# Two token mixers: softmax scaling on ScalarE, softmax steps by column, and the S5 states' products in another place and order

## The chip, the cores and the metric

The kernel runs on one core of a Trainium2 chip, as one program with one launch. The metric is the device time of one execution in microseconds. The profile records one execution on the chip: what each engine ran, when, and what it waited for. The engines are TensorE (PE in the profile, its weight loads PEld), VectorE (DVE), ScalarE (ACT), GpSimd (POOL) and SyncE (SP), which here only issues transfers.

## The reference

A trunk of two layers works on 256 latent tokens and 256 context tokens of 1024 features. Each layer is a SwiGLU half-step, a token mixer, and another SwiGLU half-step, each between two RMS norms with a shift, a scale and a gate from a conditioning vector. Only the latent tokens are returned, so the second layer computes less for the context. The mixer is what the change touches:

```
q, k, v, u, gb, gc, z = split(h @ w_in)
# attention: 8 heads in 2 groups, window of 128 and all context, a sink per head
p = softmax(concat([s_loc, s_ctx, sink])); out = p[..., :-1] @ v
# S5: 16 groups of 64 complex states, both directions
s[t] = a * s[t-1] + B u[t];  y = Re(C s) + d * u
g = gelu(y);  ssm = g * sigmoid(g @ w_glu + b_glu)
# short convolution: gb * conv3(gc * z)
y = concat([attn, ssm, conv]) @ w_out
```

## The kernel before

Features lie on the 128 partitions, tokens along the free axis: columns 0 to 255 are context, 256 to 511 latent. Large products are made from fp32 values split into a high and a low part (`wsplit` for weights, `split` for activations): ACT casts the high part, DVE or POOL subtracts for the low part (L134, L143), and PE runs three matmuls per tile (L156).

A mixer is a list of small steps, `PROG[l]`, run in the order written by hand. PE executes in exactly that order. The other engines' instructions are ordered by a scheduler when the program is built, from its own estimate of times and from their order in the program. The steps that matter here: `t` input projection tiles, `s0`/`s1` the S5 states of group half 0 and 1 (`ssm_states`), `o` their output (`ssm_out`), `b` the way back to features with GELU (`ssm_back`), `g` the gate (`ssm_glu`), `S` scores and softmax of an attention unit (`attn_s`), `T` its transposes, which wait for the scaled probabilities, `V` the product with the values, and `e` pieces of the output projection. A unit is a pair of heads with one tile of 128 latent queries (n = 1, two columns of row statistics) or the whole context (n = 2, four columns). The first mixer has 12 units, 4 of them with four columns; the second has 8 with two.

An attention unit runs on DVE: two maxima (L1166), m, nm and es (L1170 to L1174); on ACT: an exponential for es and one for each part with its sum (L1175, L1182); then on DVE again sm, its reciprocal, and the scaling of P (L1185 to L1192). An S5 state runs: PE makes two products in PSUM (pe), ACT copies them to SBUF (tx, L1047), DVE and POOL rotate them with tables co and si (L1058 to L1060, POOL into one tile tz), DVE scans (L1063), and DVE and POOL rotate back (L1068 to L1075). POOL can't read PSUM. POOL also subtracts the low parts of the output projection's weights (L134) and runs parts of the convolution (L1265 to L1273).

PSUM tiles of 128x512 come from two pools, `mm` with six banks (scores S, pe, projections, gate) and `ms` with two. The tables co, si and rho of each state (tiles tvv and tt) are loaded by SP's queue, which also carries all weights, in order.

Of the kernel before, what the change touches and what calls it, by code (L numbers as in the profile page):

```python
# [12 lines left out]
AF = mybir.ActivationFunctionType  # L13
OP = mybir.AluOpType
# [14 lines left out]
SCALE = 64 ** -0.5  # L29
# [49 lines left out]
class Trunk:  # L79
# [140 lines left out]
    def setup2(self):  # L220

        nc, a = self.nc, self.a
        self.ropec = self.cst("ropec", [128, 2, 256])
        nc.sync.dma_start(self.ropec, a["k_rope"])
        tri = self.slot("tri")[:, :256].rearrange("p (i c) -> p i c", i=2)
        nc.sync.dma_start(tri, a["k_tri"])
        self.misc = self.cst("misc", [128, NL, 24])
        nc.sync.dma_start(self.misc, a["misc"])
        self.par = self.cst("par", [128, 3, NL * 16])
        nc.sync.dma_start(self.par, a["ssm_par"])  # L230
        self.ssmd = self.cst("ssmd", [128, NL, 4])
        nc.sync.dma_start(self.ssmd, a["ssm_d"])
        self.mask16 = self.cst("mask16", [128, 16])
        nc.sync.dma_start(self.mask16, a["k_mask16"])
        self.ij = self.cst("ij", [64, 128])
        nc.sync.dma_start(self.ij, a["k_ij"])
        self.trib = self.cst("trib", [128, 2, 128], BF16)
        nc.vector.tensor_copy(self.trib, tri)
        bg = self.misc[:, :, 16:18]
        nc.vector.tensor_scalar(bg, bg, 0.5, None, op0=OP.mult)  # L240


    def conditioning(self):
# [603 lines left out]
    def ssm_tables(self, l):  # L847
# [6 lines left out]
        for gh in range(2):  # L854
# [3 lines left out]
            for i in range(3):  # L858
                self.R[l, gh, i] = dr("R", 512)

# [171 lines left out]
    def ssm_states(self, l, gh, U):  # L1032

        nc = self.nc
        v = nc.vector
        E = []
        for ri in range(2):
            w = self.wraw(self.W[l, gh, ri])
            p = self.ps("pe")
            for i in range(8):  # L1040
                for d in range(2):
                    hf = slice(64 * d, 64 * d + 64)
                    nc.tensor.matmul(p[hf, i * 64:(i + 1) * 64], w[:, i * 128 + 64 * d:i * 128 + 64 * d + 64],
                                     U[8 * gh + i][:, 64 * d:64 * d + 64], start=True, stop=True,
                                     skip_group_check=True, tile_position=(0, 64 * d))
            e = self.own("tx", 2)
            nc.scalar.activation(e, p, AF.Copy)  # L1047
            E.append(e)
        R = []
        for i in range(3):  # L1050
            r = self.own("tvv", 2) if i < 2 else self.own("tt")
            nc.sync.dma_start(r, self.R[l, gh, i])
            R.append(r)
        co, si, rho = R
        tt = [self.own("tw"), self.own("tz")]
        X = [self.own("tc"), self.own("tpw")]
        for i, (s0, s1, o) in enumerate(((0, 1, OP.add), (1, 0, OP.subtract))):
            v.tensor_tensor(tt[0], E[s0], co, op=OP.mult)  # L1058
            nc.gpsimd.tensor_tensor(tt[1], E[s1], si, op=OP.mult)
            v.tensor_tensor(X[i], tt[0], tt[1], op=o)  # L1060
        Y = [self.own(f"tbb{i}") for i in range(2)]
        for i in range(2):
            v.tensor_tensor_scan(Y[i], rho, X[i], 0.0, op0=OP.mult, op1=OP.add)  # L1063
        S = [self.slot("S") for _ in range(2)]
        z = lambda x: x.rearrange("p (g c) -> p g c", c=64)
        f, r = slice(0, 64), slice(64, 128)
        for i, (s0, s1, o) in enumerate(((0, 1, OP.subtract), (1, 0, OP.add))):
            v.tensor_tensor(tt[0], Y[s0], co, op=OP.mult)  # L1068
            nc.gpsimd.tensor_tensor(tt[1], Y[s1], si, op=OP.mult)
            s, t0, t1 = z(S[i]), z(tt[0]), z(tt[1])  # L1070
            v.memset(s[f, :, 0:1], 0.0)
            v.memset(s[r, :, 31:32], 0.0)
            v.tensor_tensor(s[f, :, 1:64], t0[f, :, 0:63], t1[f, :, 0:63], op=o)
            v.tensor_tensor(s[r, :, 30::-1], t0[r, :, 0:31], t1[r, :, 0:31], op=o)
            v.tensor_tensor(s[r, :, 63:31:-1], t0[r, :, 31:63], t1[r, :, 31:63], op=o)  # L1075
        return S
# [26 lines left out]
    def ssm_back(self, yt, lo):  # L1103

        nc = self.nc
        cl = lo // CH
        n = 64 - cl
        p = self.ps("pyt")
        pv = p.rearrange("p (c j) -> p c j", j=CH)
        for j in range(CH):  # L1110
            for q in range(128 // n):
                c = slice(n * q, n * q + n)
                nc.tensor.matmul(pv[c, cl:, j], yt[c, j * n:j * n + n], self.ident[c, c], start=True, stop=True,
                                 skip_group_check=True, tile_position=(n * q, n * q))
        g = self.slot("gelu")[:, lo:]
        x = p[:, lo:]
        nc.scalar.activation(g, x, AF.Square)
        nc.vector.tensor_scalar(g, g, 0.044715, 1.0, op0=OP.mult, op1=OP.add)
        nc.vector.tensor_tensor(g, g, x, op=OP.mult)
        nc.scalar.activation(g, g, AF.Tanh, scale=math.sqrt(2.0 / math.pi))  # L1120
        nc.vector.scalar_tensor_tensor(g, g, 1.0, x, op0=OP.add, op1=OP.mult)
        return g

    def ssm_glu(self, l, G, cat, lo):

        nc = self.nc
        wg = self.slot("wglu")
        nc.sync.dma_start(wg, self.a["w_glu"][l])
        for half in range(2):
            p = self.ps("pglu")  # L1130
            for k in range(2):
                nc.tensor.matmul(p[:, lo:], wg[:, k * 256 + half * 128:k * 256 + half * 128 + 128], G[k],
                                 start=k == 0, stop=k == 1)
            o = self.slot("sg")[:, lo:]
            nc.scalar.activation(o, p[:, lo:], AF.Tanh, bias=self.misc[:, l, 16 + half:17 + half], scale=0.25)
            nc.vector.scalar_tensor_tensor(o, o, 1.0, G[half], op0=OP.add, op1=OP.mult)
            ch, cl = self.slot("xh", F32R), self.slot("xl", F32R)
            nc.scalar.activation(ch[:, lo:], o, AF.Copy, scale=0.25)
            nc.vector.scalar_tensor_tensor(cl[:, lo:], o, 0.25, ch.bitcast(F32)[:, lo:], op0=OP.mult, op1=OP.subtract)
            cat[6 + half] = ch, cl  # L1140


    def attn_s(self, l, i, q, k, qt):
        nc = self.nc
        S = [self.ps("S") for _ in range(2)]
        for part in ((qt,) if qt is not None else (0, 1)):
            for ab in range(2):
                pr = slice(64 * ab, 64 * ab + 64)
                if qt is not None:
                    o, qo = S[ab], CTX + qt * 128  # L1150
                else:
                    o, qo = S[ab][:, part * 256:part * 256 + 256], part * 128
# [4 lines left out]
        if qt is not None:  # L1157
            c = 384 if qt == 0 else 256
# [3 lines left out]
        n = 1 if qt is not None else 2  # L1162
        w = 512 // n
        mx = self.tiny("mx", 4)
        for ab in range(2):
            nc.vector.tensor_reduce(mx[:, n * ab:n * ab + n], S[ab].rearrange("p (n k) -> p n k", n=n), axis=AX.X,  # L1166
                                    op=OP.max)
        sink = self.misc[:, l, 4 * i:4 * i + 2 * n] if n == 2 else self.misc[:, l, 4 * i:4 + 4 * i:2]
        m = self.tiny("m", 4)[:, :2 * n]
        nc.vector.scalar_tensor_tensor(m, mx[:, :2 * n], SCALE, sink, op0=OP.mult, op1=OP.max)  # L1170
        nm = self.tiny("nm", 4)[:, :2 * n]
        nc.vector.tensor_scalar(nm, m, -1.0, None, op0=OP.mult)
        es = self.tiny("es", 4)[:, :2 * n]
        nc.vector.tensor_tensor(es, sink, m, op=OP.subtract)  # L1174
        nc.scalar.activation(es, es, AF.Exp)  # L1175
        sm = self.tiny("sm", 4)[:, :2 * n]
        Pm = []
        for ab in range(2):
            P = self.slot("P")
            for z in range(n):  # L1180
                j = ab * n + z
                nc.scalar.activation(P[:, z * w:(z + 1) * w], S[ab][:, z * w:(z + 1) * w], AF.Exp, bias=nm[:, j:j + 1],  # L1182
                                     scale=SCALE, accum_out=sm[:, j:j + 1])
            Pm.append(P)
        nc.vector.tensor_tensor(sm, sm, es, op=OP.add)  # L1185
        rd = self.tiny("rd", 4)[:, :2 * n]
        nc.vector.reciprocal(rd, sm)
        for ab in range(2):
            for z in range(n):
                j = ab * n + z  # L1190
                o = Pm[ab][:, z * w:(z + 1) * w]
                nc.vector.tensor_scalar(o, o, rd[:, j:j + 1], None, op0=OP.mult)  # L1192
        return Pm

    def attn_t(self, Pm, qt):
# [436 lines left out]
```

## Time and profile before

| | us |
|---|---|
| median of 3 runs | 1827.9 (1822.71 to 1828.61) |
| the profiled execution | 1825.46 |
| its span, first to last instruction | 1823.6 |
| TensorE busy in it | 1718.3 |
| VectorE busy in it | 1140.4 |

The first mixer lies at about 480 to 680 us of the span, the second at about 1480 to 1625. Busy time of an engine includes the time in which an instruction that has begun is held up by another engine. A row of a timeline gives the start in us, the duration in us, the engine, the line of the kernel, the operation, the tile written and the tiles read, and in brackets the idle time of the engine before it and what ended it. A row of waits says which instruction waited for which, how long in total, how often and the longest. A row of windows gives the stretch and its length, then the busy us (and instructions) of PE, PEld, DVE, ACT and POOL, the granted clock of TensorE as a share of full speed, the share of DMA in use and GB/s.

### The profile page before, as it was taken

The numbers are of one execution on the slowest core, as the hardware profiler recorded it, in microseconds if no ns is written. First come the engines' busy times: TensorE is split into PE (matmuls) and PEld (weight loads), VectorE is DVE, ScalarE is ACT, GpSimd is POOL, SyncE is SP. The second block draws the span as 40 slices with busy tenths as digits, with TensorE's granted clock in tenths as the row PEclk, the third lists the DMA queues.
The fourth block names the chain that finished last, engine by engine and source line by source line (L and its number), as shares of the span: only waits on it lengthen the run. The fifth ranks groups of instructions, "written<-read, shape, count | busy, mean of one in ns | idle before, by whom it ended". The sixth has DMA issues, their size and how long they took to land.

```text
span 1823.6 us, 28595 instructions
## 1 busy us (share of the span) xinstructions
PE 1718.3 (94%) x11040; PEld 1477.6 (81%) x11040; DVE 1140.4 (63%) x2209; ACT 660.9 (36%) x1173; POOL 712.6 (39%) x623
## 2 busy tenths in 40 slices
PE   7999988999997989999999999999999988889998
PEld 5887776899975889787888999888888977679997
DVE  5798786737489666787774276765365576852223
ACT  4332222234335454323222243422222443545443
POOL 4100886864444143553438343000001562435552
PEclk9999998999998999999999999999999999899999
DMA  7676555644144031656664332646367434445552
GB/s 281 224 226 182 187 176 175 216 146 130 36 145 145 24 93 54 199 181 204 182 193 157 91 116 81 231 139 197 115 209 233 130 104 133 147 138 186 184 186 92
DMA packets 103481, 285.94 MB, mean 157 GB/s; under 512 B 19904, under 2 KB 27152, under 8 KB 103344
## 3 DMA queue, kind: packets, MB, share of 16 engines
q1 hardware_dynamic: 102992, 283.91, 49.4%
q8 instruction: 87, 1.43, 0.3%
q14 instruction: 50, 0.41, 0.1%
q0 software_dynamic: 64, 0.12, 0.0%
q10 hardware_dynamic: 288, 0.07, 0.0%
HBM read 270.45 MB, written 15.70 MB: 157 GB/s over the span
## 4 chain that ended last, share of the span: by engine, by line
PE 70%; DVE 13%; DMA 5%; issue 5%; POOL 4%; ACT 3%; SPq 0%; DVEq 0%; ACTq 0%; POOLq 0%
PE pgu L156 33%; PE pd L156 17%; PE sk L156 7%; PE yr L493 4%; DMA wr<-in_w_ada_dram 4%; PE po L156 2%; DVE junk L249 2%; DVE wl L134 2%; ACT wh L131 1%; PE pgu L544 1%; DMA wr<-in_wgu_dram 1%; PE O L1218 1%; PE ss L341 1%; ACT hh L369 1%; DVE tn L367 1%
## 5 line engine op out<-in xcount | busy, mean ns | idle before, releaser
L134 POOL TENSOR_TENSOR wl<-wr,wh 128x1024 fp32r<-128x1024 f32 (+1 forms) x140 | 326.3, 2347 | 681.7 <-ACT wh L131 299.1
L131 ACT ACTIVATE wh<-wr 128x1024 fp32r<-128x1024 f32 (+2 forms) x350 | 342.2, 983 | 628.6 <-PE pgu L156 167.0
L156 PE MATMUL pgu<-hh,wh 128*128 128x512 f32 (+1 forms) x1296 | 468.7, 362 | 0.0
L156 PE MATMUL pgu<-hl,wh 128*128 128x512 f32 (+1 forms) x1296 | 464.9, 359 | 0.2 <-DVE hl L1473 0.2
L156 PE MATMUL pgu<-hh,wl 128*128 128x512 f32 (+1 forms) x1296 | 464.9, 359 | 0.0
L249 DVE SCALAR_TENSOR_TENSOR junk<-wr,sb 128x1024 bf16<-128x1024 f32 x224 | 312.4, 1395 | 162.3 <-DMA wr<-in_w_ada_dram 160.1
L134 DVE TENSOR_TENSOR wl<-wr,wh 128x1024 fp32r<-128x1024 f32 (+1 forms) x210 | 250.4, 1195 | 70.6 <-ACT wh L131 69.5
L156 PEld LDWEIGHTS pgu<-hh,wh 128*128 128x128 f32 x1296 | 244.6, 189 | 40.4 <-issue 1.7
L156 PEld LDWEIGHTS pgu<-hl,wh 128*128 128x128 f32 x1296 | 244.5, 189 | 39.4 <-DVE hl L1473 0.5
L156 PEld LDWEIGHTS pgu<-hh,wl 128*128 128x128 f32 x1296 | 244.4, 189 | 39.0
L156 PE MATMUL pd<-xh,wh 128*128 128x512 f32 (+1 forms) x696 | 243.5, 350 | 6.9 <-ACT xh L617 6.9
L156 PE MATMUL pd<-xl,wh 128*128 128x512 f32 (+1 forms) x696 | 239.3, 344 | 1.4 <-DVE xl L618 1.4
L156 PE MATMUL pd<-xh,wl 128*128 128x512 f32 (+1 forms) x696 | 239.0, 343 | 0.0
L156 PEld LDWEIGHTS pd<-xh,wh 128*128 128x128 f32 x696 | 132.6, 190 | 25.1 <-ACT xh L617 8.2
L156 PEld LDWEIGHTS pd<-xl,wh 128*128 128x128 f32 x696 | 132.4, 190 | 19.3 <-DVE xl L618 2.7
L156 PE MATMUL sk<-hh,wh 128*128 128x256 f32 x480 | 141.2, 294 | 6.2 <-ACT hh L369 6.2
L156 PE MATMUL sk<-hl,wh 128*128 128x256 f32 x480 | 139.8, 291 | 6.8 <-DVE hl L372 6.8
L156 PEld LDWEIGHTS pd<-xh,wl 128*128 128x128 f32 x696 | 132.4, 190 | 16.1
L156 PE MATMUL sk<-hh,wl 128*128 128x256 f32 x480 | 138.9, 289 | 0.0
L156 PEld LDWEIGHTS sk<-hl,wh 128*128 128x128 f32 x480 | 94.6, 197 | 8.5 <-DVE hl L372 8.3
L156 PEld LDWEIGHTS sk<-hh,wh 128*128 128x128 f32 x480 | 94.6, 197 | 7.9 <-ACT hh L369 7.8
L617 ACT ACTIVATE xh<-pgu 128x512 fp32r<-128x512 f32 (+1 forms) x61 | 35.1, 575 | 169.8 <-DVE pgu L616 169.5
(375 smaller groups left out, 2474.1 us busy)
## 6 DMA issues: line engine op xcount, KB each, us to landing
wr<-in_wgu_dram SPq DMA_DIRECT2D x170, 512.0 KB, 4.2
wr<-in_w_ada_dram SPq DMA_DIRECT2D x144, 512.0 KB, 4.3
wr<-in_wd_dram SPq DMA_DIRECT2D x72, 320.0 KB, 3.2
wr<-in_w_in_dram SPq DMA_DIRECT2D x32, 512.0 KB, 3.9
wr<-in_wd_dram SPq DMA_DIRECT2D x36, 448.0 KB, 3.5
wr<-in_wdr_dram SPq DMA_DIRECT2D x22, 512.0 KB, 3.7
wr<-in_w_out_dram SPq DMA_DIRECT2D x10, 512.0 KB, 4.6
V<-tvv SPq DMA_DIRECT2D x16, 256.0 KB, 2.5
```

Of the source, the lines that this page charges most:

```text
L131: nc.scalar.activation(h[:, :cols], w[:, :cols], AF.Copy)
L134: eng.tensor_tensor(lo[:, :cols], w[:, :cols], h.bitcast(F32)[:, :cols], op=OP.subtract)
L156: mm = lambda a_, x_, st, sp: nc.tensor.matmul(po, a_[:, c], x_[:, lo:hi], start=st, stop=sp, skip_group_check=True)
L249: self.nc.vector.scalar_tensor_tensor(self.junk, w, 1.0, self.sb[:, s], op0=OP.mult, op1=OP.mult, accum_out=self.mod[l][:, m, b, s:s + 1])
L341: self.nc.tensor.matmul(p[:, b:b + 1], t[:, lo + b * 128:lo + (b + 1) * 128], self.rf[:, 0:1], start=first and b == 0, stop=last, skip_gro ...
L367: nc.vector.scalar_tensor_tensor(sc[d % 3], self.x[d][:, lo:hi], self.gs[l][s_][:, d, s:s + 1], rb[:, :hi - lo], op0=OP.mult, op1=OP.mult)
L369: nc.scalar.activation(H[d][0][:, lo:hi], sc[d % 3], AF.Identity, bias=bs[d])
L493: mm = lambda x_, a_, st, sp: self.nc.tensor.matmul(p, x_[:, c], a_[:, o:o + 512], start=st, stop=sp, skip_group_check=True)
L544: nc.tensor.matmul(ps[i // 2][:, o:o + 128], w[:, k * 128:k * 128 + 128], U[k][:, t * 128:t * 128 + 128], start=t + n + i % 2 == 0, stop=n ...
L617: nc.scalar.activation(gh[:, lo:hi], pu, AF.Copy)
L1218: nc.tensor.matmul(O[pr, :w], vt[:, kt * 128 + 64 * ab:kt * 128 + 64 * ab + 64], PT[ab][:, kt * w:(kt + 1) * w], start=kt == 0, stop=kt == ...
```

## The change

In `attn_s` the sinks are negated once at set-up; nm is made directly as the smaller of -SCALE times the maximum and the negated sink, es as nm minus that, and nm, es and sm are made column by column with per-row operands. es is exponentiated after the probabilities, and the probabilities are multiplied by the reciprocal sum on ACT. In `ssm_states` POOL makes both of its first products in two tiles, DVE multiplies co into the products in PSUM and combines there; the rotation back runs for the imaginary part first, with two pairs of tiles, and POOL's product stands first. In `ssm_back` the constant of the GELU is folded into the square, so that one DVE pass less is left, and in `ssm_glu` the gate is worked out in PSUM.

```diff
@@ setup2
         nc.vector.tensor_scalar(bg, bg, 0.5, None, op0=OP.mult)
+        sk = self.misc[:, :, :16]
+        nc.vector.tensor_scalar(sk, sk, -1.0, None, op0=OP.mult)
@@ ssm_states
             nc.scalar.activation(e, p, AF.Copy)
             E.append(e)
+            pe.append(p)
...
         tt = [self.own("tw"), self.own("tz")]
         X = [self.own("tc"), self.own("tpw")]
-        for i, (s0, s1, o) in enumerate(((0, 1, OP.add), (1, 0, OP.subtract))):
-            v.tensor_tensor(tt[0], E[s0], co, op=OP.mult)
-            nc.gpsimd.tensor_tensor(tt[1], E[s1], si, op=OP.mult)
-            v.tensor_tensor(X[i], tt[0], tt[1], op=o)
+        for i in range(2):
+            nc.gpsimd.tensor_tensor(tt[i], E[1 - i], si, op=OP.mult)
+        for i, o in enumerate((OP.add, OP.subtract)):
+            v.tensor_tensor(pe[i], pe[i], co, op=OP.mult)
+            v.tensor_tensor(X[i], pe[i], tt[i], op=o)
...
-        for i, (s0, s1, o) in enumerate(((0, 1, OP.subtract), (1, 0, OP.add))):
-            v.tensor_tensor(tt[0], Y[s0], co, op=OP.mult)
-            nc.gpsimd.tensor_tensor(tt[1], Y[s1], si, op=OP.mult)
+        for i, o, tags in ((1, OP.add, ("tw", "tz")), (0, OP.subtract, ("tc", "tpw"))):
+            tt = [self.own(t) for t in tags]
+            nc.gpsimd.tensor_tensor(tt[1], Y[1 - i], si, op=OP.mult)
+            v.tensor_tensor(tt[0], Y[i], co, op=OP.mult)
@@ ssm_back
-        nc.scalar.activation(g, x, AF.Square)
-        nc.vector.tensor_scalar(g, g, 0.044715, 1.0, op0=OP.mult, op1=OP.add)
-        nc.vector.tensor_tensor(g, g, x, op=OP.mult)
+        nc.scalar.activation(g, x, AF.Square, scale=math.sqrt(0.044715))
+        nc.vector.scalar_tensor_tensor(g, g, 1.0, x, op0=OP.add, op1=OP.mult)
@@ ssm_glu
-            o = self.slot("sg")[:, lo:]
-            nc.scalar.activation(o, p[:, lo:], AF.Tanh, bias=self.misc[:, l, 16 + half:17 + half], scale=0.25)
+            o = p[:, lo:]
+            nc.scalar.activation(o, o, AF.Tanh, bias=self.misc[:, l, 16 + half:17 + half], scale=0.25)
@@ attn_s
-        m = self.tiny("m", 4)[:, :2 * n]
-        nc.vector.scalar_tensor_tensor(m, mx[:, :2 * n], SCALE, sink, op0=OP.mult, op1=OP.max)
-        nm = self.tiny("nm", 4)[:, :2 * n]
-        nc.vector.tensor_scalar(nm, m, -1.0, None, op0=OP.mult)
-        es = self.tiny("es", 4)[:, :2 * n]
-        nc.vector.tensor_tensor(es, sink, m, op=OP.subtract)
-        nc.scalar.activation(es, es, AF.Exp)
...
+        for c in cols:
+            nc.vector.tensor_scalar(nm[:, c], mx[:, c], -SCALE, sink[:, c], op0=OP.mult, op1=OP.min)
+        for c in cols:
+            nc.vector.tensor_scalar(es[:, c], nm[:, c], sink[:, c], None, op0=OP.subtract)
+        Pm = [self.slot("P") for _ in range(2)]
+        part = lambda j: Pm[j // n][:, j % n * w:j % n * w + w]
+        for j in range(2 * n):
+            nc.scalar.activation(part(j), S[j // n][:, j % n * w:j % n * w + w], AF.Exp, bias=nm[:, j:j + 1],
+                                 scale=SCALE, accum_out=sm[:, j:j + 1])
+        nc.scalar.activation(es[:, :2 * n], es[:, :2 * n], AF.Exp)
+        for c in cols:
+            nc.vector.tensor_scalar(sm[:, c], sm[:, c], es[:, c], None, op0=OP.add)
...
-                nc.vector.tensor_scalar(o, o, rd[:, j:j + 1], None, op0=OP.mult)
+        for j in range(2 * n):
+            nc.scalar.activation(part(j), part(j), AF.Copy, scale=rd[:, j:j + 1])
```

## Rows read from the trace of the kernel before

**Rows 1.** Page, part 1: busy time of each engine over the span.

```profile
PE 1718.3 (94%) x11040; PEld 1477.6 (81%) x11040; DVE 1140.4 (63%) x2209; ACT 660.9 (36%) x1173; POOL 712.6 (39%) x623
```

**Rows 2.** Windows: the two mixers' middles, and the stretch after the first.

```profile
520.00:600.00 80.00, 62.68 (x519) 49.02 (x518) 73.96 (x136) 35.29 (x89) 37.63 (x21) 0.89 0.39 128
600.00:660.00 60.00, 58.15 (x498) 51.33 (x496) 37.20 (x102) 29.29 (x74) 10.46 (x5) 1.00 0.11 35
1520.00:1606.00 86.00, 73.86 (x799) 59.09 (x798) 68.49 (x145) 40.11 (x95) 37.43 (x22) 0.90 0.54 172
```

**Rows 3.** Waits of PE, 480 to 720: total us, times, longest.

```profile
PE O L1218 <- ACT PT L1207: 8.1, 2, 5.0
PE S L1155 <- DVE xl L143: 4.5, 1, 4.5
...
PE po L156 <- DVE cl L1224: 1.8, 1, 1.8
PE pt L1202 <- DVE P L1192: 1.8, 2, 1.0
```

**Rows 4.** Waits of PE, 1480 to 1640.

```profile
PE pw L156 <- ACT wi L1237: 2.6, 1, 2.6
...
PE S L1155 <- DVE yt L1100: 2.4, 1, 2.4
PE pxr L436 <- ACT bt L423: 2.2, 1, 2.2
PE O L1218 <- ACT P L1182: 1.9, 1, 1.9
...
PE pt L1202 <- DVE P L1192: 1.0, 1, 1.0
```

**Rows 5.** Timeline of DVE, first mixer: start, us, instruction.

```profile
574.09 0.68 DVE L1121 SCALAR_TENSOR_TENSOR gelu<-gelu,pyt 128x512 f32<-128x512 f32 x1
574.68 1.72 DVE L1170 SCALAR_TENSOR_TENSOR m<-mx,misc 128x2 f32<-128x2 f32 x1
576.43 2.27 DVE L1172 TENSOR_SCALAR nm<-m 128x2 f32<-128x2 f32 x1
...
590.38 0.17 DVE L1172 TENSOR_SCALAR nm<-m 128x4 f32<-128x4 f32 x1
```

**Rows 6.** Timeline of POOL, the same stretch.

```profile
571.67 7.00 POOL L134 TENSOR_TENSOR wl<-wr,wh 128x1024 fp32r<-128x1024 f32 x3 [7.17 <-ACT wh L131]
```

**Rows 7.** Groups of DVE by form, 514 to 600, then 1520 to 1600.

```profile
L1192 DVE TENSOR_SCALAR P<-P,rd 128x256 f32<-128x256 f32 x16 | 7.6, 537 | 0.1
...
L1192 DVE TENSOR_SCALAR P<-P,rd 128x512 f32<-128x512 f32 x6 | 2.6, 482 | 0.1
...
L1192 DVE TENSOR_SCALAR P<-P,rd 128x512 f32<-128x512 f32 x16 | 8.4, 568 | 0.1
```

**Rows 8.** Groups of ACT by form, whole span.

```profile
L1182 ACT ACTIVATE P<-S,nm 128x512 f32<-128x512 f32 x32 | 21.9, 684 | 25.6 <-DVE es L1174 18.1 <-DVE nm L1172 4.6 <-PE O L1218 2.9
...
L1182 ACT ACTIVATE P<-S,nm 128x256 f32<-128x256 f32 x16 | 7.4, 472 | 1.7 <-DVE es L1174 1.7
```

**Rows 9.** Timeline of DVE, and all instructions of L322 (ns min/median/max): column steps.

```profile
681.60 0.33 DVE L322 TENSOR_SCALAR rd<-t 128x1 f32<-128x1 f32 x2
...
L322 DVE TENSOR_SCALAR rd<-t x32: 201/206/214, 418.0 to 1489.1; 128x1 f32<-128x1 f32 x32
```

**Rows 10.** Timelines of DVE and POOL: first products of the states.

```profile
517.15 1.78 DVE L1058 TENSOR_TENSOR tw<-tx,tvv 128x512 f32<-128x512 f32 x1
...
519.81 2.21 POOL L1059 TENSOR_TENSOR tz<-tx,tvv 128x512 f32<-128x512 f32 x1 [1.42 <-DVE tc L1060]
```

**Rows 11.** Timelines of ACT and DVE, second mixer.

```profile
1549.08 0.36 ACT L1237 ACTIVATE wi<-pw 128x256 f32<-128x256 f32 x1
...
1549.82 0.60 ACT L1047 ACTIVATE tx<-pe 128x512 f32<-128x512 f32 x1
...
1553.91 0.67 DVE L1060 TENSOR_TENSOR tc<-tw,tz 128x512 f32<-128x512 f32 x1
```

More of the change, by code (lines that the diff above doesn't have):

```diff
@@ L1035, in ssm_states @@
         v = nc.vector
-        E = []
+        E, pe = [], []
         for ri in range(2):
@@ L1168, in attn_s @@
         sink = self.misc[:, l, 4 * i:4 * i + 2 * n] if n == 2 else self.misc[:, l, 4 * i:4 + 4 * i:2]
-        m = self.tiny("m", 4)[:, :2 * n]
-        nc.vector.scalar_tensor_tensor(m, mx[:, :2 * n], SCALE, sink, op0=OP.mult, op1=OP.max)
-        nm = self.tiny("nm", 4)[:, :2 * n]
-        nc.vector.tensor_scalar(nm, m, -1.0, None, op0=OP.mult)
-        es = self.tiny("es", 4)[:, :2 * n]
-        nc.vector.tensor_tensor(es, sink, m, op=OP.subtract)
-        nc.scalar.activation(es, es, AF.Exp)
[L1176 to L1185, printed above, removed]
-        rd = self.tiny("rd", 4)[:, :2 * n]
[L1187 to L1191, printed above, removed]
-                nc.vector.tensor_scalar(o, o, rd[:, j:j + 1], None, op0=OP.mult)
+        cols = [slice(j, j + 1) for j in range(2 * n)]
+        nm, es, sm = (self.tiny(t, 4) for t in ("nm", "es", "sm"))
+        for c in cols:
[10 more added lines that the diff above has]
+            nc.vector.tensor_scalar(sm[:, c], sm[:, c], es[:, c], None, op0=OP.add)
+        rd = self.tiny("rd", 4)[:, :2 * n]
+        nc.vector.reciprocal(rd, sm[:, :2 * n])
+        for j in range(2 * n):
+            nc.scalar.activation(part(j), part(j), AF.Copy, scale=rd[:, j:j + 1])
         return Pm
```

## The prediction

> **What bounds the kernel now.** I read the page first. TensorE (PE) is busy for 94% of the span and every other engine for 63% or less [rows 1], so over the whole kernel time can only be won where PE stands still. The mixers are the only code that the change touches, so the windows view of their middles came next [rows 2]. There the picture turns over: from 520 to 600 DVE is busy 73.96 of 80 us and PE only 62.68; from 1520 to 1606 DVE 68.49 and PE 73.86 of 86. PE is thus idle 17.3 and 12.1 us, at a granted clock of 0.89 and 0.90. From 600 to 660 it is idle 1.85 us at 1.00: there is nothing to win there. These 29.5 us are the ceiling of what the change can give by closing waits.
>
> The view of PE's waits names what ends them. In the first mixer nearly all come from the two engines that the change relieves or loads [rows 3]: PT copies on ACT (8.1, in two waits), a split xl on DVE (4.5), a split cl (1.8), the scaled P (1.8). In the second they are smaller and mixed [rows 4]: a copy wi (2.6), yt (2.4), bt (2.2, the rows step, which the change doesn't touch), P on ACT (1.9), the scaled P (1.0).
>
> The timelines of DVE and POOL show why DVE is so full. At 574.68 the step m on 128x2 takes 1.72 us and nm at 576.43 takes 2.27, though a wide nm at 590.38 takes 0.17 [rows 5]. Between 571.67 and 578.67 POOL runs three weight splits [rows 6]; m ends where the second one should, nm where the third does. In the same stretch the DVE operation at 574.09 with one operand in PSUM takes its plain 0.68. So in this trace DVE operations on SBUF operands alone wait for POOL operations to end, and one with a PSUM operand does not.
>
> **The change part by part.**
>
> *Probabilities scaled by ACT.* In the two stretches DVE gives up 7.6 + 2.6 = 10.2 us and 8.4 us [rows 7]. ACT takes the same tiles. No row shows a scaled copy with a per-row factor; nearest are the exponentials on the same shapes with a per-row bias, 684 and 472 ns [rows 8], which I take. That adds 16 x 0.472 + 6 x 0.684 = 11.7 us to ACT's 35.29 of 80, and 16 x 0.684 = 10.9 to its 40.11 of 86 [rows 2, 7]: still under 60% busy. If the factor cost nothing beyond a copy, it would be less, but a gain in ACT time over today is excluded.
>
> *Small steps by column.* m goes, and the negation of the sinks is done once at set-up. nm, es and sm become one instruction per column with a per-row operand. Two such column steps elsewhere take 0.33 us together [rows 9], so one costs what an unstretched wide one does, 0.17 [rows 5]. A unit with two columns goes from four wide steps to six column steps, one with four columns to twelve, so without POOL in the way DVE loses 2 x 0.17 = 0.33 and 8 x 0.17 = 1.3 us per unit. With 4 four-column and 3 two-column units in the first stretch that is +6.2 us; with 8 two-column units in the second, +2.6. Against it stand the stretched steps. The pair of rows 5 loses 1.72 + 2.27 - 0.3 = 3.7 us, a second pair like it stands at 583 to 587, and the second stretch has one nm like it and three shorter ones: 7 and 4 us. If single-column steps are not stretched, DVE's time barely moves, -0.8 and -1.4, but the loss goes from the places where PE waits; the other bound is that they are stretched as well, and then DVE pays the 6.2 and 2.6 on top. None of the 32 instructions of that line is longer than 0.214 us [rows 9], so I take the first.
>
> *States, first products.* Now two products of one row pair go to POOL back to back into separate tiles, and DVE multiplies in PSUM. Before, the second product on POOL waited for DVE to free the one tz (1.42 us idle) [rows 10], and DVE's product took 1.78 where a two-input operation of that shape takes 0.67 [rows 11]: two of the first mixer's four are stretched like this and three of the second's, by less: 2.2 and 1.9 us. With a PSUM operand I expect 0.68 each [rows 5].
>
> *States, second products.* The cross product that needs only the first scan is now first on POOL, and the two results have separate tiles. No work goes away; the chain of each state shortens by about the wait for the tile, 1.4 us or more, and R's next transfer on SP, which waits for the tiles of the last state to be read, moves up with it.
>
> *GELU and gate.* One DVE pass of four goes, two instructions per mixer at no more than the 0.48 us of rows 7, so 0.9. The gate now works in PSUM; its bank is held a little longer, at no cost while PE has the output projection to run, which fills it from 600 to 660 [rows 2]; without that cover it would cost the three passes that now read the bank, 3 x 0.68 us by rows 5.
>
> DVE's sum: 10.2 + 0.8 + 2.2 + 0.9 = 14.1 of 73.96 us, and 8.4 + 1.4 + 1.9 + 0.9 = 12.6 of 68.49. DVE then falls to about 60 and 56 us, below PE's own 62.68 and 73.86. It stops being the bound, and what is late next are the round trips between engines.
>
> So the gain goes wait by wait. First mixer: xl stands behind stretched state work, 2.5 of 4.5; scaled P, 1.5 of 1.8, since ACT is the emptier engine there; the two PT waits, 2 of 3.1 (ACT was held by a convolution tile that waited for DVE) and 3 of 5.0 (the stretched pair); cl 1.5 of 1.8. That is 10.5; I take 8, because POOL's splits then stretch other two-input work, and because each unit's way gets longer by a hand-over: es after both exponentials, one more column, ACT 2 x 0.684 against DVE 2 x 0.48, some 0.5 us. Second mixer: yt 1.5, P and scaled P 1.5, wi 1: 4 in all. Together 12. The profiled execution took 1825.46 us (span 1823.6 and 1.9 around it), 2.4 below the median of the runs; 1825.5 - 12 gives 1813.5, and I say 1813.
>
> **The rivals.**
>
> *The hand-over eats it (about the same).* If every one of the 15 units in the two stretches stands on PE's path, 15 x 0.5 = 7.5 us come back, and ACT's queue, in order, holds weight casts behind a factor that DVE owes. Gain 12 - 7.5, or 1821. The Trainium skill, ScalarE: Activation LUTs, section Rules for kernel authors, speaks for this: it would leave multiplications to VectorE rather than ScalarE. By it the move should cost; rows 7 and 8 agree on the price per tile, 684 against 482 ns. Against it: DVE is the full engine here and ACT the half-empty one.
>
> *Held banks (slower).* The states' products now sit in the mm pool, six banks, until X is made; before, a copy freed them. At S2 of the second mixer the program has t9 waiting for its copy, S3 with two banks and s1 with two, and wants two more: seven of six. PE already waits 2.6 us there for wi [rows 4]. If no X comes earlier, the bank is free not after the copies of about 1545 to 1550 but after X at 1553.91 + 0.67 = 1554.6 [rows 11], 5 us after the 1549.4 at which PE now goes on; with a second place like it in the first mixer, 10 us. Less 4 that survive of the gain: 1831. It decides from the point where X is made no more than 2 us earlier than now.
>
> *All idle time closes.* If round trips hide, the whole 29.5 us less bt's 2.2 and some 3 of hand-over goes: 1801. A clock of 1.00 in these stretches would add to it; I count none.
>
> *The lock only moves.* POOL's work is unchanged, so scans, splits and second products can take the stretching that the small steps lose. The Trainium skill, SBUF — State Buffer, section Who interferes with whom, says that whichever of the two starts first keeps the shared pair for its whole instruction. That is what rows 5 and 6 look like. Gain 6 instead of 12, 1819.
>
> **How the numbers follow.** A change under 0.3%, 5.5 us, is about what a measurement of this kernel can't tell from none; it parts the first two cases from the hand-over. Forecast, a gain of 8 to 20: 0.45. The lock moves: 0.12. All idle closes: 0.13. Hand-over: 0.19. Held banks: 0.11. So faster 0.70, same 0.19, slower 0.11. The range leaves out the far half of the best case and most of the worst: 1802 to 1827.
>
> **What would show it.** In the profile after: DVE under 63 us busy from 520 to 600 or its counterpart and PE's idle there about 9 instead of 17; no small softmax step over 0.4 us; PT waits under 4 us; ACT scale at 0.6 to 0.7 us per 512 columns. A wait of PE for a state's X, or for a scaled P of several us, would prove me wrong, as would an order on ACT in which weight casts stand behind the scales.

## The result and the profile after

The changed kernel takes 1805.99 us (median, 1804.59 to 1807.65) against 1827.16 of the kernel before on the same chip. The ratio of the two is 0.9896, 95% interval 0.988 to 0.9911. By the ratio that is 19 us less, by the two medians 21; 12 to 14 were forecast. The profiled execution has a span of 1804.8 us. The number lies inside the range of 1802 to 1827, 4 us above its lower end; most of the reasons for it turn out to be wrong.

Part 1 of the page of the changed kernel, to be laid beside [rows 1]:

```profile
PE 1702.1 (94%) x11040; PEld 1456.6 (81%) x11040; DVE 1109.0 (61%) x2222; ACT 686.8 (38%) x1221; POOL 717.1 (40%) x623
```

PE's *busy* time fell by 16.2 us with the same 11040 matmuls. A change that only closes waits would be expected to shorten the idle time instead, and that went from 105.3 to 102.7 us only.

The same three windows as [rows 2], each moved to where its work now lies (columns as there):

```profile
512.30:592.30 80.00, 64.11 (x518) 49.33 (x517) 59.70 (x148) 44.89 (x111) 36.09 (x20) 0.87 0.38 130
592.30:652.30 60.00, 57.58 (x498) 51.03 (x496) 33.23 (x102) 36.91 (x88) 11.20 (x5) 1.00 0.11 36
1505.30:1591.30 86.00, 74.01 (x810) 58.73 (x810) 56.97 (x142) 49.73 (x112) 37.84 (x22) 0.92 0.53 173
```

DVE was relieved as forecast, by 14.3 and 11.5 us. PE's idle time in the first window is 15.9 us, where it was 17.3 and 9 was expected. DVE stopped being the bound, and little came of it.

Waits of PE in the changed kernel, 494 to 636.2 (first mixer), against [rows 3]:

```profile
PE pt L1202 <- ACT P L1192: 6.0, 2, 3.6
PE S L1160 <- DVE xl L143: 5.1, 1, 5.1
PE O L1218 <- ACT PT L1207: 3.5, 2, 2.2
PE py L1100 <- DMA wr<-V: 1.2, 1, 1.2
```

And 1466 to 1622 (second mixer), against [rows 4]:

```profile
PE S L1160 <- DVE tpw L1065: 5.3, 1, 5.3
...
PE pxr L438 <- ACT bt L425: 2.3, 1, 2.3
PE pt L1202 <- ACT PT L1207: 1.4, 1, 1.4
PE py L1100 <- DMA wr<-V: 1.3, 1, 1.3
PE pt L1202 <- ACT P L1192: 1.1, 1, 1.1
```

The waits on PT, cl, wi and yt shrank or went. In their place PE now waits for the scaled P on ACT (6.0 instead of 1.8 on DVE) and, in the second mixer, for a state's X (tpw), whose product holds a PSUM bank. Both were named beforehand as what would prove the forecast wrong. From the first `ut` to the first `ss` behind it, the first mixer got 0.6 us shorter (142.8 to 142.2); from `ut` to the first `ph`, the second got 2.7 shorter (106.6 to 103.9). The other 15.5 us of the 18.8 came from stretches whose code the change doesn't touch. What became shorter there is the step from one matmul to the next. Timeline of PE in a boundary, the kernel before, at a granted clock of 1.00 (start, duration, instruction):

```profile
423.80 0.28 PE L156 MATMUL pd<-xh,wh 128*128 128x256 f32 x1
423.91 0.28 PE L156 MATMUL pd<-xl,wh 128*128 128x256 f32 x1
...
424.98 0.28 PE L156 MATMUL pd<-xl,wh 128*128 128x256 f32 x1
```

Matmuls of the same product in the changed kernel, at 1.00 as well:

```profile
420.29 0.28 PE L156 MATMUL pd<-xh,wl 128*128 128x256 f32 x1
420.40 0.28 PE L156 MATMUL pd<-xh,wh 128*128 128x256 f32 x1
...
421.42 0.28 PE L156 MATMUL pd<-xh,wh 128*128 128x256 f32 x1
```

Ten steps from start to start take 1.18 us in one and 1.13 in the other. Nothing waits in either stretch and the operations are the same.

### The profile page after: what moved, and what is told of

It reads as the page before. It is cut to its first block, busy times and chain, and to the rows that moved or that the text cites. A ratio compares the mean times of both kernels' runs of the same rounds, so it can differ in the third digit from the quotient of the medians.

```text
span 1804.8 us, 28662 instructions
## 1 busy us (share of the span) xinstructions
PE 1702.1 (94%) x11040; PEld 1456.6 (81%) x11040; DVE 1109.0 (61%) x2222; ACT 686.8 (38%) x1221; POOL 717.1 (40%) x623
## 4 chain that ended last, share of the span: by engine, by line
PE 68%; DVE 12%; DMA 9%; issue 5%; ACT 3%; POOL 2%; SPq 0%; DVEq 0%; ACTq 0%; POOLq 0%
PE pgu L156 31%; PE pd L156 15%; PE sk L156 8%; DMA wr<-in_w_ada_dram 5%; PE yr L495 4%; DVE junk L251 4%; PE po L156 3%; DVE wl L134 2%; PE pw L156 2%; ACT wh L131 1%; PE pgu L546 1%; DMA wr<-in_wd_dram 1%; PE S L1160 1%; PE ss L343 1%; PE pt L1202 1%
```

## The experiments

Two theories. *Work* (theories A and W below): the gain is work and waits taken from the mixers. *Place* (theory P): without `m`, one small tile in two buffers less, 64 bytes per partition, the weight tiles begin 64 bytes lower, and that sets the step between matmuls. Place was found after the first four runs, which still name a theory B (a shift in the set-up) and a theory C (scatter between executions). The first table gathers all runs. Weights and activations are the bytes by which these tiles begin higher than before. Steps are means over the starts of consecutive matmuls of the one line that makes all split products, 7,964 pairs in each trace: narrow are those under 160 ns (256 columns), wide those of 200 to 300 (mostly 512 columns). Sum is over all pairs, also the 107 to 124 of 300 ns and more (waits, or 512 columns at the lower clock). Mixers is the sum of the two spans named above. The ratio is to runs of the kernel before on the same chip.

| kernel | weights | activations | narrow ns | wide ns | sum us | mixers us | ratio (95%) |
|---|---|---|---|---|---|---|---|
| before | 0 | 0 | 119.0 | 231.6 | 1432.6 | 249.4 | 1 |
| e1 set-up instruction | 0 | 0 | 119.0 | 232.1 | 1428.1 | 249.4 | 0.9989 (0.9979 to 1.0) |
| e2 softmax part | -64 | 0 | 116.1 | 232.5 | 1420.1 | 250.9 | 0.9938 (0.9922 to 0.9954) |
| e3 states part | 0 | 0 | 118.8 | 231.6 | 1432.2 | 247.5 | 0.9999 (0.9986 to 1.0012) |
| e4 GELU and gate part | 0 | 0 | 118.9 | 231.6 | 1428.9 | 251.7 | 1.0002 (0.999 to 1.0014) |
| e5 before, m in place | -64 | 0 | 115.0 | 232.5 | 1416.7 | 248.8 | 0.9926 (0.9908 to 0.9943) |
| e6 changed, 64 bytes | 0 | 0 | 119.0 | 231.6 | 1430.4 | 245.1 | 0.998 (0.9966 to 0.9993) |
| e7 changed, 32 bytes | -32 | 0 | 118.0 | 233.2 | 1433.4 | 248.2 | 0.9997 (0.9984 to 1.001) |
| changed | -64 | 0 | 115.9 | 232.6 | 1416.7 | 246.1 | 0.9896 (0.988 to 0.9911) |
| e8 es in place | -128 | 0 | 119.8 | 226.5 | 1416.1 | 246.2 | 0.9916 (0.9895 to 0.9936) |
| e9 scaling on DVE | -64 | 0 | 115.5 | 232.4 | 1420.1 | 255.6 | 0.9944 (0.9929 to 0.996) |
| e10 activations moved | -64 | +64 | 119.8 | 226.5 | 1417.8 | 247.7 | 0.9926 (0.9911 to 0.994) |
| e11 no rott | -192 | 0 | 117.1 | 228.8 | 1413.7 | 246.8 | 0.9908 (0.9893 to 0.9923) |
| e12 wide steps | -64 | 0 | 114.7 | 232.5 | 1414.8 | 250.5 | 0.9944 (0.9926 to 0.9962) |

**e1: the set-up instruction alone.**

```diff
+        sk = self.misc[:, :, :16]
+        nc.vector.tensor_scalar(sk, sk, 1.0, None, op0=OP.mult)
```

> The kernel before, plus the one set-up instruction of the change, with the factor 1.0 instead of -1.0: the sinks keep their values, nothing else differs. Theory A (the gain is work taken from the mixers): the time stays that of before, within 2 us, and the start of mixer 0 (first ut, 501.7 us before, 494.0 after) stays near 501.7. Theory B (the gain of 15 us outside the mixers comes from a shift in the set-up that changes how the long stretches of equal code fall): 6 us or more are won, and mixer 0 starts near 494. Theory C (the stretches outside the mixers differ from one execution to the next, whatever the kernel): the time stays within 2 us of before, yet the start of mixer 0 lies away from 501.7 by several us in either direction.

The time stays. In its profile mixer 0 starts at 498.2 us instead of 501.7. In e3 and e4, which are identical to before up to that point, it starts at 502.3 and 498.5. So up to some 4 of the 7.7 us that the changed kernel has won by then can be scatter between executions. Theory B falls; C can account for a part.

**e2, e3, e4: one part each.** The diff of the change, cut to `attn_s` with the set-up, to `ssm_states`, and to `ssm_back` with `ssm_glu`.

> The kernel before with the softmax part of the change alone (columns, scale on ScalarE, sinks negated at set-up). By the prediction's steps this part carries most of the gain (12.5 of the 18 us of waits that close): 8 us faster, won in the mixers. By theory B it wins at least what the set-up instruction alone wins, 6 us or more, and about nothing between ut and ss of mixer 0, where the whole change won 0.6 us. If the hand-over to ScalarE eats the gain, the mixers themselves get slower by 0 to 4 us.

> The kernel before with the states' part alone. By the prediction's steps: 2 to 4 us faster, between ut and ss of each mixer, from second products that no longer wait for a tile. By the held banks: 0 to 5 us slower, with a wait of PE for an X in mixer 1 (5.3 us for the change as a whole). By theory B: the start of mixer 0 stays at 501.7 us, since nothing ahead of it changes, and no gain stands outside the mixers.

> The kernel before with the GELU and gate part alone: two DVE passes fewer in each mixer, the gate in PSUM. By the prediction's steps: 0 to 1 us faster. By theory B nothing ahead of mixer 0 moves, and the time stays within 2 us. If stretches of equal code behind a mixer gain or lose with the time at which they begin, this kernel moves by several us with hardly a change inside the mixers.

States and GELU alone give nothing. The softmax part wins 11 us, but its two mixers are together 1.5 us longer than before; its sum of steps is 12.5 us shorter. It is the one of the four without `m`. The states alone make a trade that the whole change does not show, a shorter first mixer against a longer second: mixer 0 139.4 instead of 142.8, mixer 1 108.1 instead of 106.6. In that second mixer of e3 PE waits 7.2 us for wi, where before it waited 2.6 [rows 4], and it never waits for an X, which the held banks would have shown:

```profile
PE S L1159 <- ACT wi L1241: 7.2, 1, 7.2
```

**e5: the kernel before with m in place.** No operation is added or removed.

```diff
-        m = self.tiny("m", 4)[:, :2 * n]
+        m = mx[:, :2 * n]
```

> The kernel before, except that m is written over the row maxima instead of into a tile of its own. No instruction is added or taken away; the one thing that goes is the small tile m, in two buffers, 64 bytes per partition in front of the weight tiles, which all begin 64 bytes lower, as they do in the changed kernel and in the run with the softmax part alone. Theory P (place: where the weight tiles lie sets the step from matmul to matmul, 119 to 124 ns in before and 113 to 119 ns in the two kernels without m, over some 7,900 matmuls of that line): 8 to 11 us faster, the boundary stretch between the norm's first two sums 18.5 us instead of 19.1, the stretch of the output projection behind mixer 0 13.8 instead of 15.2. Theory W (the gain is work and waits taken from the mixers): within 2 us of before, 19.1 and 15.2.

13.5 us faster (interval 10 to 17) with before's own operations, and PE's waits in the first mixer are about those of before: 9.4 us for PT (8.1 before), 4.4 for xl, 1.8 for cl. PE's busy time is 1701.8 us, as in the changed kernel, and in e6 below it is back at 1715.5. Theory W can't give this.

The two named stretches were 18.5 and 13.3 us. The first lies at a granted clock of 1.00 and shows the place. The second doesn't: its clock was 0.87 in e5 and 0.78 in before, and e9 and e12, with the weights where e5 has them, took 14.8 and 14.9 at 0.77. Nor does the clock make the whole gain. Over the span it was 0.973 to 0.976 in e5's runs and 0.968 to 0.977 in before's 23 beside them, and counted at a clock of 1.00 alone the steps are 118.9 ns for 256 columns and 232.5 for 512 in before, 115.0 and 233.3 in e5.

**e6, e7: the changed kernel, weights moved back by 64 and by 32 bytes.**

```diff
         self.small = P("small", 2)
+        self.pad = P("pad", 1).tile([128, 16], F32, name="pad")
```

(8 instead of 16 for e7.)

> The changed kernel with 64 unused bytes per partition between the small tiles and the weight tiles, so that the weights lie where they lay before the change; the same instructions. Theory P: 8 to 11 us slower than the changed kernel, so 1813 to 1817 on the scale on which before is 1824, with the step of 119 to 124 ns back. Theory W: the time of the changed kernel, 1803 to 1806.

> The changed kernel with 32 unused bytes in the same place: the weights begin at a multiple of 64 bytes, which they do in none of the other kernels. Theory P gives no sign of its own: between the changed kernel and the one with 64 bytes, 0 to 11 us slower, if the place acts step by step; faster than the changed kernel, if what counts is a multiple of 64. Theory W: the time of the changed kernel.

With the weights where they lay before, the whole change is worth 0.2%, 3.6 us (1.3 to 6.2); the place is worth more than theory P said. With 32 bytes the whole change is worth nothing (0.9997), so a multiple of 64 is no help. The groups of matmuls `sk`, which all have 256 columns (ns min/median/max), show the same difference. Before:

```profile
L156 PE MATMUL sk<-hh,wh x480: 278/282/775, 443.1 to 1511.2; 128*128 128x256 f32 x160
```

Changed:

```profile
L156 PE MATMUL sk<-hh,wh x480: 276/276/582, 438.6 to 1496.6; 128*128 128x256 f32 x160
```

e6, the changed kernel with 64 bytes ahead of the weights:

```profile
L157 PE MATMUL sk<-hh,wh x480: 274/282/775, 440.3 to 1507.2; 128*128 128x256 f32 x160
```

**e8, e10, e11: other distances.** e8 writes es over the maxima (`es = mx`); e10 adds to e8 the same 64 bytes, ahead of the pool `slots`; e11 keeps `rott` in `t[:, 496:512]`.

> The changed kernel with es written over the row maxima, so that one more small tile goes and the weights lie another 64 bytes lower, 128 below before. Theory P with a period of 128 bytes: back to the step of before, 8 to 11 us slower than the changed kernel. Theory P without such a period: the time of the changed kernel or better. Theory W: the time of the changed kernel.

> The changed kernel with es written over the row maxima and 64 unused bytes in front of the activation tiles: the weights lie where they lie in the changed kernel, the activations, which PE streams past them, 64 bytes higher. Their distance is that of the run with es over the row maxima. If the weights' own place sets the step: as in the changed kernel, 113 and 117 ns for 256 columns, 231 and 236 for 512. If the distance between the two sets it: as in that run, 120 and 226 to 227. If the activations' place counts by itself: a third pattern.

> The changed kernel with one small tile of the S5 set-up (rott, 128 bytes in two buffers) kept in a corner of a larger tile instead: the weights lie 128 bytes lower than in the changed kernel, 192 below before, the activations stay. If the step repeats with 128 bytes: 113 and 117, 231 and 236 ns as in the changed kernel and its time within 2 us, with the run 64 bytes above it as the other phase. If it doesn't: another pattern, by the runs so far anywhere from 10 us faster to 18 us slower than the changed kernel.

e10 has the changed kernel's weight addresses, yet its steps are others. It has e8's distance between weights and activations, and its mean steps are e8's. Timeline of PE in e8:

```profile
421.08 0.28 PE L156 MATMUL pd<-xh,wh 128*128 128x256 f32 x1
421.20 0.28 PE L156 MATMUL pd<-xl,wh 128*128 128x256 f32 x1
421.32 0.28 PE L156 MATMUL pd<-xh,wl 128*128 128x256 f32 x1
```

And in e10:

```profile
420.83 0.28 PE L157 MATMUL pd<-xh,wh 128*128 128x256 f32 x1
420.95 0.28 PE L157 MATMUL pd<-xl,wh 128*128 128x256 f32 x1
421.07 0.28 PE L157 MATMUL pd<-xh,wl 128*128 128x256 f32 x1
```

120 ns in both, with two different weight addresses, where the changed kernel has 113 in this stretch. So it is the distance between the two operands that acts, at least in this pair, the only one that tests it. The stretch between the norm's first two sums, at a clock of 1.00 in every trace, sorts all fourteen kernels by distance (weights less activations): 19.05 to 19.09 us in the five at 0, 19.07 at -32, 18.49 in all five at -64, 19.21 in both at -128 (e8, e10), 18.93 at -192. It doesn't repeat with 128 bytes: e11 is neither the changed kernel nor before. Each distance trades narrow matmuls against wide ones: e8 has the slowest narrow and the fastest wide ones and its interval overlaps those of e11 and the changed kernel. None of the tried distances beats the changed kernel beyond its interval.

**e9: scaling back on DVE, columns kept.**

```diff
-            nc.scalar.activation(part(j), part(j), AF.Copy, scale=rd[:, j:j + 1])
+            nc.vector.tensor_scalar(part(j), part(j), rd[:, j:j + 1], None, op0=OP.mult)
```

> The changed kernel with the probabilities scaled by DVE again, the columns and all else kept; every tile lies where it lies in the changed kernel, so the place of the weights is out of the comparison. By the prediction's steps DVE takes its 10.2 and 8.4 us back and the mixers lose what the hand-over to ACT had won: 3 to 6 us slower than the changed kernel. By the rival (the hand-over eats it; PE waits 6.0 us for scaled P and 3.5 for PT copies in mixer 0 of the changed kernel, both on ACT): 2 to 5 us faster, with P's waits under 2 us. Either is small beside the 12 us of the place.

The rival falls: the mixers are 9.5 us longer than the changed kernel's (8.9 longer than the mean of the six kernels with its mixers), and the ratio is 0.005 worse. The forecast's price was too small. Timeline of DVE in e9, four scalings in a row:

```profile
563.35 6.90 DVE L1192 TENSOR_SCALAR P<-P,rd 128x256 f32<-128x256 f32 x4
```

And POOL in the same stretch:

```profile
562.78 7.06 POOL L134 TENSOR_TENSOR wl<-wr,wh 128x1024 fp32r<-128x1024 f32 x3 [7.58 <-ACT wh L131]
```

Three of the four take 1.94, 2.43 and 2.43 us instead of some 0.5 [rows 7]: each is held until one of POOL's splits ends. PE's waits for P in that mixer (PE, 496.2 to 642.5):

```profile
PE pt L1202 <- DVE P L1192: 10.4, 4, 4.7
```

**e12: the small steps wide again, scaling kept on ACT.**

```diff
+        k = slice(0, 2 * n)
-        for c in cols:
-            nc.vector.tensor_scalar(nm[:, c], mx[:, c], -SCALE, sink[:, c], op0=OP.mult, op1=OP.min)
-        for c in cols:
-            nc.vector.tensor_scalar(es[:, c], nm[:, c], sink[:, c], None, op0=OP.subtract)
+        nc.vector.scalar_tensor_tensor(nm[:, k], mx[:, k], -SCALE, sink, op0=OP.mult, op1=OP.min)
+        nc.vector.tensor_tensor(es[:, k], nm[:, k], sink, op=OP.subtract)
...
-        for c in cols:
-            nc.vector.tensor_scalar(sm[:, c], sm[:, c], es[:, c], None, op0=OP.add)
+        nc.vector.tensor_tensor(sm[:, k], sm[:, k], es[:, k], op=OP.add)
```

> The changed kernel with the small softmax steps wide again: one DVE instruction each for nm, es and sm of a unit instead of one per column (three instead of six, or instead of twelve); probabilities still scaled on ACT, all tiles where the changed kernel has them. By the prediction's steps: in the stretches 520 to 600 and its like of the second mixer DVE loses 6.2 and 2.6 us of column steps but gets steps held up by POOL of 1.7 to 2.3 us back (3.7 us per pair), in places where PE waits; 2 to 4 us slower than the changed kernel. If the columns are only a cost (24 more DVE instructions of 0.2 us in the first mixer's middle): 1 to 4 us faster. The run with the scaling on DVE, which kept the columns, stands at 0.9944 of before, 9 us behind the changed kernel's 0.9896; if that gap is the columns' doing and not the scaling's, it closes here too.

Slower than the changed kernel: 4.4 us in the mixers, just over the 2 to 4 forecast, and more in the ratio (0.9944 to 0.9896, with 2.7 us between their intervals). Timeline of DVE in e12, while POOL runs three splits from 565.25 to 572.24:

```profile
567.68 2.29 DVE L1179 TENSOR_TENSOR es<-nm,misc 128x2 f32<-128x2 f32 x1
570.23 2.03 DVE L1186 TENSOR_TENSOR sm<-sm,es 128x2 f32<-128x2 f32 x1 [0.27 <-ACT es L1185]
```

And of DVE in the changed kernel, while POOL runs the same splits from 564.51 to 571.54:

```profile
567.62 0.33 DVE L1180 TENSOR_SCALAR es<-nm,misc 128x1 f32<-128x1 f32 x2
569.71 0.34 DVE L1188 TENSOR_SCALAR sm<-sm,es 128x1 f32<-128x1 f32 x2 [1.76 <-ACT es L1186]
```

By column two instructions take 0.33 and 0.34 us; wide, one takes over 2. The Trainium skill, SBUF — State Buffer, section Who interferes with whom, lists the scalar form among the operations that can take the shared pair of ports. The scalings of e9 and the nm of [rows 5] agree with it; the scalar form on a single column is never held in the traces of the changed kernel, e6 and e9, 144 instructions each. In the changed kernel 26 of them run wholly inside a two-input POOL operation.

## Why the prediction was right in its number and wrong in its reasons

- **The step that failed** is the first: "over the whole kernel time can only be won where PE stands still" [rows 1], and with it the sum's nothing outside the mixers. Busy time is not time at full rate. Some 13.5 of the 19 us are a shorter step between matmuls while PE is busy (e5), by a change of address that the prediction never priced: the line of the diff that drops `m` was read as an instruction removed, not as 64 bytes removed. That the forecast of 12 still lands near the 19 is luck: a term that it didn't have made up for one that it had too large. The 13.5 of e5 and the 3.6 of e6 make some 17. The rest may be the clock's, which is not shown: the changed kernel's four runs had 0.977 to 0.979, before's profiled execution 0.974, and among the 23 runs of before beside e5 a run with 0.001 less took about 1 us longer.
- **The sum of 12 us in the mixers** was mis-sized. Six kernels with the changed mixers (changed, e6, e7, e8, e10, e11) have a mean of 246.7 us there, three with those of before (before, e1, e5) 249.2: 2.5 us, and e6 puts the whole change without the place at 3.6. Wait by wait in the first mixer: PT lost 4.6 (forecast 5), cl 1.8 (1.5), but xl gained 0.6 (forecast a loss of 2.5) and P gained 4.2 (forecast a loss of 1.5).
- **P's wait** comes from ACT's queue, as in the hand-over rival, but in the other order: the rival had weight casts held behind a scale, and here a scale stands behind a weight cast. The queue of ACT in the changed kernel:

```profile
558.53 1.37 ACT L1192 ACTIVATE P<-P,rd 128x512 f32<-128x512 f32 x2
559.75 0.42 ACT L1105 ACTIVATE yt<-py 128x256 f32<-128x256 f32 x1
560.01 0.43 ACT L1223 ACTIVATE ch<-O 128x256 fp32r<-128x256 f32 x1
560.28 1.11 ACT L131 ACTIVATE wh<-wr 128x1024 fp32r<-128x1024 f32 x1
561.23 0.68 ACT L1125 ACTIVATE gelu<-gelu 128x512 f32<-128x512 f32 x1
561.74 1.74 ACT L1192 ACTIVATE P<-P,rd 128x256 f32<-128x256 f32 x4
```

  The second set's factor was made at 559.91 on DVE (0.18 us), and the set starts at 561.74, with ch, a weight cast and a gelu between: 1.65 us in the queue, of the 3.6 that PE waits here. The rival's price is there, its sign isn't: on DVE, PE waits longer for P (e9).
- **xl** shows the rival "the lock only moves". DVE in the changed kernel, which has no gap here:

```profile
515.88 1.73 DVE L1075 TENSOR_TENSOR tw<-tbb,tvv 128x512 f32<-128x512 f32 x1
517.53 1.78 DVE L1075 TENSOR_TENSOR tc<-tbb,tvv 128x512 f32<-128x512 f32 x1
519.23 2.88 DVE L143 TENSOR_TENSOR xl<-wi,xh 128x512 fp32r<-128x512 f32 x1
...
523.05 1.50 DVE L1081 TENSOR_TENSOR S<-tc,tpw 64x256 f32<-64x256 f32 x1
...
526.64 2.29 DVE L134 TENSOR_TENSOR wl<-wr,wh 128x1024 fp32r<-128x1024 f32 x1
528.85 0.68 DVE L143 TENSOR_TENSOR xl<-wi,xh 128x512 fp32r<-128x512 f32 x1
```

  And POOL:

```profile
517.02 1.73 POOL L1074 TENSOR_TENSOR tz<-tbb,tvv 128x512 f32<-128x512 f32 x1
518.71 2.85 POOL L134 TENSOR_TENSOR wl<-wr,wh 128x1024 fp32r<-128x1024 f32 x1
```

  The last xl, which ends PE's wait, takes 0.68; the one at 519.23 takes 2.88, until 0.55 us after POOL's split, and the second products ahead of it 1.73 and 1.78, as the first ones did [rows 10]. That is 4.3 us of delay in DVE's queue. The operations at 523.05 and 526.64, beside other POOL work, take 1.50 and 2.29 where their like takes 0.42 and 1.22, so 6.5 in all, more than the wait of 5.1.
- **Right, with sizes:** DVE's relief, 14.1 and 12.6 forecast, 14.3 and 11.5 measured; columns never stretched (144 instructions, none over 0.22 us; one alone takes 0.206, but two in a row 0.33, as assumed); PT's waits under 4 us. The scale on ACT is dearer than the 684 and 472 ns of [rows 8]:

```profile
L1192 ACT ACTIVATE P<-P,rd 128x512 f32<-128x512 f32 x32 | 21.5, 725 | 3.9 <-DVE rd L1190 3.7
L1192 ACT ACTIVATE P<-P,rd 128x256 f32<-128x256 f32 x16 | 6.9, 519 | 1.0 <-DVE rd L1190 1.0
```

- **Neither softmax edit pays without the other.** The forecast priced them one by one. Without either (e9, e12) 9.5 and 4.4 us come back in the mixers: the wide DVE work on SBUF alone that then stands in the softmax takes the lock's loss. Both together, without the rest of the change, win nothing in the mixers either (e2, 1.5 us longer).
- **Held banks:** the wait for X is there in the second mixer, 5.3 us, the price that was forecast for that place; the like of it in the first mixer didn't come. Mixer 1 is shorter all the same: the waits for wi (2.6), yt (2.4) and the P of `O` (1.9) [rows 4] are gone. A version with the first products in SBUF was not run, so what the bank costs by itself stays open.

By itself the forecast's mechanism would have ended at about 0.998, a gain too small to be told from none by its own bound.

## What to carry to other kernels

PE at 94% busy is not PE at 94% of its best: compare the step from matmul to matmul, at one granted clock, before calling a stretch full. A removed or added tile moves every tile behind it, so an edit is tested against a kernel in which a pad puts the addresses back. When two engines lock each other out, as DVE and POOL do here, relieving one instruction can hand the loss to the next one in line, so edits are tested as a set and not only one by one.

## What the runs showed of the hardware that was not expected

- The step between matmuls whose weights and activations come from SBUF depends on where the two lie, and in the one pair that tests it (e8, e10) on how far apart they are: at the five distances tried, 115 to 120 ns for 256 columns and 227 to 234 for 512, counted at a clock of 1.00 and in the same order. Over this kernel the sums, waits included, differ by up to 19.7 us (1413.7 to 1433.4). The Trainium skill, TensorE: Matmul & The Clock Gate, section Step-by-step: what each phase is for, has weights and streamed operand come through two ports of their own, so that loading one takes nothing from the other. By that the distance should not matter; e5, e6, e8 and e10 say that the place does matter, and the measurement decides. Why it does, and which of the two reads gives way, stays open: no run separates the weight load from the stream.
- A DVE scaling with a per-row factor has a median of 0.48 us and took up to 2.66 beside POOL's splits (e9), while instructions on one column kept to 0.22.
